# Seven-product matmuls for two output projections, with new sequence cuts, in a hybrid decoder block

## Chip, cores, metric

One Trainium2 chip, all 8 cores, one launch. The metric is the device time of the slowest core in microseconds (us). The time is in most executions within 0.3% of the median; in some a whole die runs at a lower granted clock, and such a run is called slow.

Four names of kinds of core are used throughout, because the program is a switch over four variants: cores 0/4, 1/5, 2/6 and 3/7 compute the first, second, third and last quarter of a sequence, for batch 0 (cores 0 to 3) and batch 1 (cores 4 to 7). A later quarter has more keys to attend to, so it gets fewer tokens. Which quarter is how long is set by the constant `CUTS`.

## The reference, cut

```python
# D_MODEL 2048, SEQ 4096 + 16 meta tokens, 8 heads of 128, conv width 1024, D_FF 8192
xn = rms_norm(h, norm_mix)
q, k, v, fg, cb, cc, cx, gl = split(xn @ w_in)         # one combined projection
a = forgetting_attention(rms(q), rms(k), v, log_sigmoid(fg + b)) @ w_attn_out   # 1024 -> 2048
c = (cb * short_conv(cc * cx, conv_w)) @ w_conv_out                             # 1024 -> 2048
ga, gc = split(sigmoid(gl + b_gate))                   # two gates of 2048
h = h + (ga * a + gc * c) @ w_o
h = h + square(relu(rms_norm(h, norm_mlp) @ w_up)) @ w_down
```

## The kernel before

Each core runs through these stages: projections for q, k, v; attention; convolution; gates together with the two output projections; `w_o` (called `o`); and the MLP. All large products with an inner width of 2048 or more already use a seven-product scheme of the Strassen kind: a product of 2x2 blocks is made of 7 block products in place of 8, for some sums of weights (`wsum`) and of operands (`lincomb`), which VectorE makes in f16. The two output projections, whose inner width is 1024, were plain: four quadrant products of 8 matmuls per pair of column blocks, called `plain` below.

```python
CUTS = [0, 1200, 2264, 3240, L]
...
def lincomb(nm, kb, extra=()):          # operand sums, on VectorE
    def sub(out, a, b, w=()): S.op("dve", lambda e: e.tensor_tensor(..., op=ALU.subtract), ...)
    return [lambda: sub(JT3, J22, J12[nm]), lambda: sub(JT1, J12[nm], J11, ...),
            lambda: sub(JT2, J22, JT1), lambda: sub(JT4, J21, JT2)]

def taps(j):                            # depthwise convolution of width 3
    S.op("act", lambda e: e.activation(out=y[:], in_=ub[:, 0:n + 2], func=AF.Identity, scale=cw(0)), ...)
    for t in (1, 2):
        S.op("dve", lambda e, t=t: e.scalar_tensor_tensor(out=y[:], in0=ub[:, t:t + n + 2], scalar=cw(t), in1=y[:], ...), ...)
...
groups7 += [("g", "xn", kG(p, g), (g, p)) for p in range(8) for g in range(2)]     # gates
groups7 += [("o", "m7", K_O + 2 * p, (0, p)) for p in range(8)]
...
class Group:
    def P1(self): self.prod(self.X, self.wa[:, 0:8], [self.ka], J11, True); self.copy(p1_t, p1k)
    def P7(self): self.sprod(self.Y, 3, JT3, True)      # sprod: a product with a weight sum
    def P6(self): self.sprod(self.X, 2, JT2, False); self.copy(us_t, usk)
    def P2(self): self.prod(self.Z, self.wa[:, 8:16], [self.ka], J21, True)
    ...                                                 # P5, P3, P4 likewise
    def plain(self, q, sl=None):
        def mm(e):
            for x in range(NP):
                for kb in range(8):
                    rhs = cT[kb][:, lo:lo + fw] if g else aT[:, kb, q0 + lo:q0 + lo + fw]
                    ins = e.matmul(ps[sl[x]][:, 0:fw], lhsT=w[:, 8 * s + kb, :], rhs=rhs, start=(kb == 0), stop=(kb == 7))
        S.op("pe", mm, ...)
        tt_op(wide(sv_[g]), pv(sl, fw), wide(sv_[g]), ALU.mult, ...)       # gate times product
        if g: tt_op(operand["m7"](j, p), sv_[0], sv_[1], ALU.add, ...)     # the two branches
...
def fin(self, s, half):                 # stage o: operand and square of a finished row
    S.op("act", lambda e: e.activation(out=operand["x7"](j, self.b), in_=ht, func=AF.Identity, ...), ...)
    S.op("act", lambda e: e.activation(out=sq2[q][:], in_=ht, func=AF.Square), ...)
    pend.append(ssq)                    # the matmul that sums the squares is put off
def flush(keep):
    while len(pend) > keep: pend.pop(0)()
```

`NP` is 2 on cores 0, 1, 4, 5, whose rows are split in two matmuls, and 1 on the others. A solver places all tiles in the on-chip memory; tiles that find a place early (`soon`) can be filled while attention still runs.

Of the kernel before, what the change touches and what calls it, by code (L numbers as in the profile page):

```python
# [14 lines left out]
L = SEQ + NMETA  # L15
# [9 lines left out]
CUTS = [0, 1200, 2264, 3240, L]  # L25
# [3 lines left out]
WMAX = 1200  # L29
W0 = 490  # L30
NTW = 24 + 48 + 16 + 128
K_G, K_O, K_F, NR = 24, 72, 88, 6
# [236 lines left out]
T_V, T_K, T_ATT, T_C0, T_G, T_GE, T_OE, T_END = 12, 14, 16, 20, 24, 30, 35, 99  # L269

def solve(want, busy, movable, hpair):
# [4 lines left out]
    for it in range(400):  # L276
        used = list(busy)

        def put(nb, t0, t1):
            live = sorted((a, b) for a, b, s0, s1 in used if s0 < t1 and t0 < s1)  # L280
            x = O_A
            for a, b in live:
                if x + nb <= a:
                    break
                x = max(x, b)
            if x + nb > TOP:
                return None
            used.append((x, x + nb, t0, t1))
            return x
        place, soon = {}, set()  # L290
        for w in first + sorted(rest, key=lambda w: -prio[w[0]]):
            x = put(w[3], movable[w[0]], w[5]) if w in first and w[0] in movable else None
            if x is not None:
                soon.add(w[0])
            else:
                x = put(w[3], w[4], w[5])
            if x is None:
                prio[w[0]] *= 1.5
                break
            place[w[0]] = x  # L300
# [23 lines left out]
def emit(nc, sems, T, psall, ps, G, S0, g0):  # L324
# [155 lines left out]
    for h in range(H):  # L480
        S.reg(("QT", h), "QT", o_Q + h * 2 * W, o_Q + (h + 1) * 2 * W)
        for c in range(nch):
# [10 lines left out]
    busy = [(O_A, o_A1, 0, T_C0), (o_A1, o_rs, 0, T_C0), (o_rs, o_xog, 0, 9), (o_xog, o_R, 0, T_GE), (o_R, o_H, 0, T_V), (o_wk, o_wk + 32768, 0, T_K),  # L493
            (o_K, o_Q, 0, T_ATT), (o_K, o_K + 4096, 0, T_C0), (o_Q, o_end, 0, T_GE)] + ([(o_x, o_V, 0, T_K), (o_V, o_K, 0, T_ATT)] if early else [(o_x, o_K, 0, T_ATT)])
    J11, J21, J22, JT1, JT3, JT2, JT4 = range(7)
    BASE, EXT = (J11, J21, J22, JT1), (JT3, JT2, JT4)
    NSS, NZ, NSQ = 6, 3, 3
# [3 lines left out]
    J12 = {nm: 7 if nm == "xn" and apart else JT1 for nm in ("xn", "m7", "x7", "u7")}  # L501
# [3 lines left out]
    def ask(name, shape, dtype, t0, t1, keys):  # L505

        want.append((name, shape, dtype, r32(int(np.prod(shape)) * (2 if dtype in (BF16, F16) else 4)), t0, t1, keys))
    f32s = lambda nm, k, w, t0, t1: [ask("%s%d" % (nm, i), [w], F32, t0, t1, [(nm, i)]) for i in range(k)]
    op7 = lambda nm, x, w, js, t0, t1: [ask("%s%s%d_%d" % (nm, x, kb, j), [w], F16, t0, t1, [(nm, j, kb)]) for kb in range(8) for j in js]
    ask_h = lambda i: [ask("hp%d_%d" % (i, s), [n], F32, T_GE, T_END, [("hp", i, s, c) for c in range(2)]) for s in range(2)]  # L510
    for i in range(NR):
        ask("ring%d" % i, [2048], F16, T_V, T_END, [("ring", i)])
    f32s("ub", 1, 2 * TC, T_K, T_G)
    f32s("yb", 1, n + 2, T_K, T_G)
    f32s("cx", 2, TC, T_K, T_G)
    op7("xn", "e", TC, EXTX, T_ATT, T_GE)
    ask("yb1", [n + 2], F32, T_S, T_G, [("yb", 1)])
    for i in range(NSS):
        ask("swt%d" % i, [8, 128], F16, T_S, T_END, [("swt", i)])
    for nm in ("p1", "us", "tt"):  # L520
        f32s(nm, 1, TC, T_S, T_END)
    for j in range(8):
        ask("cT%d" % j, [n + 2], F16, T_S if j < 2 or apart else T_C0, T_GE, [("cT", j)])
    for g in range(2):
        f32s("sg%d" % g, 4, TC, T_G, T_GE)
    op7("m7", "b", TH, BASE, T_G, T_OE)
    op7("x7", "b", TH, BASE, T_GE, T_END)
    op7("x7", "e", TH, EXT, T_GE, T_END)
    op7("u7", "b", TH, BASE, T_OE, T_END)
    op7("u7", "e", TH, EXT, T_OE, T_END)  # L530
    ask("rstd_m", [n], F32, T_OE - 1, T_END, [("rstd_m", c) for c in range(2)])
    f32s("zz", NZ, TH + 8, T_GE, T_END)
    for i in range(2):
        ask_h(i)
    op7("m7", "e", TH, EXT, T_GE, T_OE)
    assert not apart or n <= 1000
    place, soon, nhp = solve(want, busy, {w[0]: T_G if w[0][:3] == "m7e" else T_K for w in want if w[0][:3] in ("m7e", "xne")}, (r32(4 * n), T_GE, T_END))
# [7 lines left out]
    soon7 = [all("xne%d_%d" % (kb, x) in soon for x in EXTX) for kb in range(8)]  # L545
    xcol = {J11: (0, c0), J12["xn"]: (0, c0 + TC), J21: (8, c0), J22: (8, c0 + TC)}
# [4 lines left out]
    operand = {nm: (lambda j, kb, nm=nm: tl["%s%s%d_%d" % (nm, "b" if j in BASE else "e", kb, j)][:]) for nm in ("m7", "x7", "u7")}  # L551
    operand["xn"] = lambda j, kb: xog[:, xcol[j][0] + kb, xcol[j][1]:xcol[j][1] + TC] if j in xcol else tl["xne%d_%d" % (kb, j)][:]
# [3 lines left out]
    rstd_m, z_t, hp = tl["rstd_m"], tls("zz", NZ), [tls("hp%d_" % i, 2) for i in range(nhp)]  # L556
    zz = lambda i: place["zz%d" % i]
    ssb = M.at("ssb", [128, TH], F32, zz(2))[0]
    S.reg("ssb", "ssb", zz(2), zz(2) + 4 * TH)
    sq2 = [M.at("sq2%d" % i, [128, TH], BF16, zz(i // 2) + i % 2 * r32(2 * TH))[0] for i in range(NSQ)]  # L560
    for i in range(NSQ):
        S.reg(("sq2", i), "sq2%d" % i, zz(i // 2) + i % 2 * r32(2 * TH), zz(i // 2) + i % 2 * r32(2 * TH) + 2 * TH)
# [592 lines left out]

    def xn_sum(kb, j):
        lincomb("xn", kb, xn_extra(kb))[j]()
        S.lastw.update({("xn", b, kb): ("dve", S.sem["dve"], S.cnt["dve"]) for b in xcol if b != JT1})
# [114 lines left out]
    plain_r = Ring([(0, 1)] if NP == 2 else [(0,), (1,), (2,), (3,)])  # L1273
    s_bank, b_bank = ((0, 1), [(0, 1), (0, 1)]) if NP == 2 else ((0,), [(1,), (2,)])

    kG = lambda p, g: K_G + (2 * g if p == 0 else 6 * p - 1 + 3 * g)
    groups7 = [(kd, "xn", 2 * i, (a, b)) for i, (kd, a, b) in enumerate(CONV) if i]
    NCV = len(groups7)
    groups7 += [("g", "xn", kG(p, g), (g, p)) for p in range(8) for g in range(2)]
# [12 lines left out]
    sw_r, z_r = Ring(list(range(NSS))), Ring(list(range(NZ)))  # L1292
    sums = {}

    def wsum(i, j):

        if i >= NG7:
            return
        k = groups7[i][2]
        assert k + 1 < wt_n[0], (i, k, wt_n[0])  # L1300
        wa, wb, ka, kb_ = wview(k), wview(k + 1), wkey(k), wkey(k + 1)
        sl = sums.setdefault(i, {})
        s = sl[j] = sw_r.next()
        t = lambda x: swt[sl[x]][:]
        a, b, op, rk = {1: lambda: (wb[:, 0:8], wb[:, 8:16], ALU.add, [kb_]),
                        2: lambda: (t(1), wa[:, 0:8], ALU.subtract, [ka, ("swt", sl[1])]),
                        3: lambda: (wa[:, 0:8], wb[:, 0:8], ALU.subtract, [ka, kb_]),
                        4: lambda: (wa[:, 8:16], t(2), ALU.subtract, [ka, ("swt", sl[2])])}[j]()
        tt_op(swt[s][:], a, b, op, rk, [("swt", s)])
# [10 lines left out]
    class Group:  # L1320
        def __init__(self, i):
# [3 lines left out]
            self.turn = (self.kind, nxt) in (("g", "o"), ("o", "u"), ("u", "d"), ("d", None))  # L1325
# [4 lines left out]
            self.cost = 8 * self.T / 2400  # L1330
            self.four = (NP == 1 and i >= NTAIL) or self.kind in ("u", "d")

        def begin(self):
            if self.four:
                self.X, self.Y, self.Z, free = slots
                if self.turn and self.kind in ("u", "o"):
# [5 lines left out]
            self.wa, self.wb = wview(self.k), wview(self.k + 1)  # L1342
            self.ka, self.kb = wkey(self.k), wkey(self.k + 1)

        def prod(self, d, w, wkeys, j, start, kbs=range(8)):
            f = self.f

            def mm(e):
                for p in range(NP):
                    for kb in kbs:  # L1350
                        ins = e.matmul(ps[d[p]][:, 0:f], lhsT=w[:, kb, :], rhs=self.op(j, kb)[:, p * f:(p + 1) * f],  # L1351
                                       start=(start and kb == 0), stop=(kb == 7), skip_group_check=not start)
# [21 lines left out]
        def up(self, src, keys, add, addk, half, j):  # L1374
            z = z_r.next()
            zk = ("zz", z)
            if add is not None:
                tt_op(wide(z_t[z][:, 0:TH]), src, wide(add[:, 0:TH]), ALU.add, keys + [addk], [zk])
                src, keys = wide(z_t[z][:, 0:TH]), [zk]
# [483 lines left out]
```

## Time and profile before

| | before |
|---|---|
| time, median of the first 5 runs | 1968.43 us (1967.19 to 2140.8) |
| TensorE busy, page of core 7 | 1891.9 us, 96% of the span |
| VectorE busy | 1227.4 us, 62% |
| ScalarE busy | 844.6 us, 43% |
| spans, cores 0 to 3 | 1911.8, 1944.8, 1942.1, 1964.3 us |

How to read it: TensorE sets the end, and the last quarter's cores are the slowest by 19 us. The prediction shows the lines for this. The view of windows has columns window, length, then busy time and instruction count of TensorE, its weight loads, VectorE, ScalarE and GpSimd, then granted clock of TensorE, DMA share and GB/s. First core 4 in its convolution stage:

```profile
334.00:521.00 187.00, 179.17 (x1423) 136.29 (x1424) 126.19 (x241) 46.94 (x72) 12.16 (x23) 0.99 0.41 68
```

TensorE is busy 179 of 187 us at a clock of 0.99. Then core 7 around the end of attention, which is at 813 us:

```profile
764.00:790.00 26.00, 24.50 (x182) 13.61 (x179) 18.75 (x50) 18.49 (x38) 1.06 (x2) 1.00 0.14 24
790.00:815.00 25.00, 21.39 (x141) 11.35 (x142) 15.93 (x28) 12.61 (x25) 1.05 (x2) 1.00 0.26 45
815.00:836.00 21.00, 15.50 (x76) 7.64 (x74) 14.59 (x41) 3.17 (x6) 1.05 (x2) 0.84 0.29 49
```

The first 51 of these 72 us run at the full clock; only after the end of attention does it fall to 0.84.

### The profile page before, as it was taken

The page shows a single profiled execution, that of the slowest core. Times are in us where ns is not written, and L with a number is a line of the kernel's source. Part 1 is how long each engine was busy: PE and PEld are TensorE (multiplying, and loading weights), DVE is VectorE, ACT ScalarE, POOL GpSimd, SP SyncE. Part 2 cuts the span into 40 slices and gives each one's busy share as a digit, 9 for nine tenths or more (in the row PEclk, how much of TensorE's full clock was granted, in tenths as well). Part 3 has the DMA queues.
Part 4 walks back from the last instruction along what each step waited for, and adds up shares of the span by engine and source line. Part 5 has one row for each costly group of instructions (what it writes and reads, how often), then busy time and mean ns, then how long its engine had stood idle before and what let it go on. Part 6 is the DMA issues. An engine that isn't in the chain of part 4 may idle for free.

```text
span 1964.4 us, 39987 instructions; the slowest of 8 cores (1911.8 to 1964.4 us)
## 1 busy us (share of the span) xinstructions
PE 1891.9 (96%) x13096; PEld 1165.0 (59%) x13096; DVE 1227.4 (62%) x2712; ACT 844.6 (43%) x1734; POOL 131.3 (7%) x254
## 2 busy tenths in 40 slices
PE   6899999999999999799999998999999999999998
PEld 2478677777777776455555554445555555555554
DVE  3534566666666655677455555667667767766765
ACT  4325667777777777322222223443113212312321
POOL 1100000000000000010000000001011001100110
PEclk9999999999999999999999999999999999999999
DMA  9840333323333314255465568866786787688676
GB/s 223 151 70 2 115 112 109 98 87 106 99 100 110 107 55 73 47 98 96 78 103 99 96 102 188 209 140 108 176 210 102 134 200 158 101 205 181 107 156 187
DMA packets 68035, 240.49 MB, mean 122 GB/s; under 512 B 7920, under 2 KB 8048, under 8 KB 67440
## 3 DMA queue, kind: packets, MB, share of 16 engines
q0 software_dynamic: 34128, 125.94, 38.3%
q1 hardware_dynamic: 33696, 111.89, 17.4%
q8 instruction: 114, 1.87, 0.4%
q14 instruction: 97, 0.79, 0.1%
HBM read 338.73 MB, written 25.00 MB: 185 GB/s over the span
## 4 chain that ended last, share of the span: by engine, by line
PE 87%; DMA 4%; DVE 3%; issue 2%; ACT 2%; SPq 0%; DVEq 0%; POOL 0%; ACTq 0%; POOLq 0%
PE ps L1351 49%; PE ps L801 12%; PE ps L837 11%; PE ps L1564 5%; PE ps L1098 5%; PE ps L1069 5%; DMA wq<-wqk 1%; DMA v_wv<-wv 1%; DMA x<-xo 1%; ACT v_PT L1084 1%; DMA v_hp<-xt 1%; DMA v_xs<-xo 0%; PE ps L1184 0%; DVE v_swt L1291 0%; ACT v_sq L1391 0%
## 5 line engine op out<-in xcount | busy, mean ns | idle before, releaser
L1084 ACT ACTIVATE v_PT<-ps,v_small 128x104 bf16<-128x104 f32 (+2 forms) x752 | 395.4, 577 | 165.2 <-PE ps L1098 86.2
L1126 DVE SCALAR_TENSOR_TENSOR v_acc<-ps,v_small,v_acc 128x387 f32<-128x387 f32 (+1 forms) x312 | 164.9, 529 | 144.4 <-PE ps L1069 106.0
L165 POOL DMA_DIRECT2D v_ring<-wB x216 | 114.0, 529 | 1708.3 <-PE ps L1351 834.5
L1069 PE MATMUL ps<-v_QT,v_KT 128*128 128x104 bf16 (+2 forms) x752 | 202.6, 281 | 10.6 <-ACT v_PT L1084 9.8
L837 PE MATMUL ps<-v_xg,v_wk 128*128 128x256 f16 (+1 forms) x1664 | 209.9, 269 | 0.5 <-DVE v_xg L996 0.5
L801 PE MATMUL ps<-v_wv,v_xg 128*128 128x387 f16 (+1 forms) x1248 | 210.0, 310 | 0.0
L1098 PE MATMUL ps<-v_VB,v_PT 128*128 128x129 bf16 (+1 forms) x1632 | 196.6, 220 | 7.2 <-DVE v_acc L1126 3.5
L1291 DVE TENSOR_TENSOR v_hp<-ps,v_hp 128x436 f32<-128x436 f32 x160 | 97.3, 608 | 135.4 <-PE ps L1351 130.5
L837 PEld LDWEIGHTS ps<-v_xg,v_wk 128*128 128x128 f16 x1664 | 150.0, 98 | 18.6 <-issue 0.6
L1382 ACT ACTIVATE v_u7b<-v_zz 128x436 f16<-128x436 f32 x128 | 72.5, 567 | 201.3 <-DVE v_zz L1380 201.3
L1098 PEld LDWEIGHTS ps<-v_VB,v_PT 128*128 128x128 bf16 (+1 forms) x1632 | 126.9, 97 | 41.0 <-issue 14.4
L1364 ACT COPY v_us<-ps 128x436 f32<-128x436 f32 (+1 forms) x99 | 51.1, 516 | 223.9 <-PE ps L1351 216.4
L801 PEld LDWEIGHTS ps<-v_wv,v_xg 128*128 128x128 f16 x1248 | 114.6, 98 | 49.9
L1351 PE MATMUL ps<-v_xne,v_swt 128*128 128x438 f16 x648 | 132.9, 348 | 2.7 <-ACT v_us L1364 1.5
L1351 PE MATMUL ps<-v_u7b,v_ring 128*128 128x436 f16 x512 | 105.4, 347 | 0.5
L1351 PE MATMUL ps<-v_x7b,v_swt 128*128 128x436 f16 x512 | 104.7, 347 | 0.9 <-ACT v_tt L1364 0.5
L1351 PE MATMUL ps<-v_u7b,v_swt 128*128 128x436 f16 x512 | 104.7, 347 | 0.8 <-ACT v_tt L1364 0.8
L1351 PE MATMUL ps<-v_x7b,v_ring 128*128 128x436 f16 x512 | 104.9, 347 | 0.0
L1351 PE MATMUL ps<-v_u7e,v_swt 128*128 128x436 f16 x512 | 104.1, 347 | 0.0
L1351 PE MATMUL ps<-v_x7e,v_swt 128*128 128x436 f16 x512 | 104.1, 347 | 0.0
L1351 PEld LDWEIGHTS ps<-v_xne,v_swt 128*128 128x128 f16 x648 | 62.2, 98 | 59.2 <-issue 6.0
L1364 ACT COPY v_tt<-ps 128x436 f32<-128x436 f32 (+1 forms) x99 | 50.9, 514 | 104.4 <-PE ps L1351 103.4
(173 smaller groups left out, 2926.6 us busy)
## 6 DMA issues: line engine op xcount, KB each, us to landing
v_ring<-wB POOLq DMA_DIRECT2D x216, 512.0 KB, 6.8
v_stage<-xe SPq DMA_DIRECT2D x52, 512.0 KB, 3.7
v_stage<-xr SPq DMA_DIRECT2D x52, 512.0 KB, 3.9
hd<-v_hp SPq DMA_DIRECT2D x40, 436.0 KB, 6.4
v_hp<-hd SPq DMA_DIRECT2D x40, 436.0 KB, 7.4
v_hp<-xt SPq DMA_DIRECT2D x16, 436.0 KB, 8.5
y<-v_hp SPq DMA_DIRECT2D x16, 436.0 KB, 5.7
wq<-wqk POOLq DMA_DIRECT2D x8, 512.0 KB, 14.4
```

Of the source, the lines that this page charges most:

```text
L165: self.eng[q].dma_start(out=out, in_=in_).then_inc(sem, 16)
L801: ins = e.matmul(ps[b][:x.shape[-1], 0:nh * 129], lhsT=x, rhs=wv_t[hg][:, kc, :], start=(kc == 0), stop=(kc == KC - 1))
L837: ins = e.matmul(ps[b][:, 0:N], lhsT=wk[:, h, kc, :], rhs=cols(kc), start=(kc == 0), stop=(kc == KC - 1))
L1069: ins = e.matmul(ps[sb][:, 0:N], lhsT=KT[ks][:, koff:koff + 128], rhs=QT[:, h, lo:hi], start=True, stop=not diag)
L1084: S.op("act", lambda e: e.activation(out=PT[pt][:m, 0:N], in_=ps[st["s"]][:m, 0:N], func=AF.Exp, bias=small[:m, bcol:bcol + 1], scale=smal ...
L1098: ins = e.matmul(ps[ob][:, k * 129:(k + 1) * 129], lhsT=PT[pt][:m, ql - lo:ql - lo + 128], rhs=Vt[vs][:m, h, :], start=(first and b == bl[ ...
L1126: S.op("dve", lambda e, ov=ov, av=av, mq=mq, fc=fc: e.scalar_tensor_tensor(out=av, in0=ov, scalar=small[:mq, fc:fc + 1], in1=av, op0=ALU.m ...
L1291: tt_op = lambda out, a, b, op, rk, wk_: S.op("dve", lambda e: e.tensor_tensor(out=out, in0=a, in1=b, op=op), reads=rk, writes=wk_)
L1351: ins = e.matmul(ps[d[p]][:, 0:f], lhsT=w[:, kb, :], rhs=self.op(j, kb)[:, p * f:(p + 1) * f], start=(start and kb == 0), stop=(kb == 7), ...
L1364: S.op("act", lambda e: e.copy(out=wide(t[:, 0:self.T]), in_=self.pv(self.X)), reads=bks(self.X), writes=[key])
L1382: S.op("act", lambda e: e.activation(out=operand["u7"](j, self.b), in_=z_t[z][:, 0:TH], func=AF.Square), reads=[zk], writes=[("u7", j, sel ...
L1564: ins = e.matmul(ps[sl[x]][:, 0:fw], lhsT=w[:, 8 * s + kb, :], rhs=rhs, start=(kb == 0), stop=(kb == 7))
```

## The change

Its intent: both output projections go through the seven-product scheme as well, 7 products of 4 matmuls per pair in place of 4 of 8, so 448 matmuls for 512 (896 for 1024 where `NP` is 2). This needs operand sums and weight sums of its own, a new memory layout (the solver gets a hand-written plan), an order of weights with all attention projections ahead of the gates, and lists that put additions off to quieter places. At the same time the sequence is cut anew, the last quarter gets 20 tokens fewer, and stage `o` may hold two squares back in place of one.

```diff
-CUTS = [0, 1200, 2264, 3240, L]
+CUTS = [0, 1216, 2280, 3260, L]
...
-    NSS, NZ, NSQ = 6, 3, 3
+    NSS, NSQ = 6, 4
...
+    op7("a7", "e", TH, EXT, T_C0, T_G, 4)
+    op7("c7", "e", TH, EXT, T_G, T_GE + 1, 4)
+    plan = [("ring", o_R)] + [("swt%d" % i, o_R) for i in range(4)] + [(x, o_R) for x in ("p1", "us", "tt", "cT1", "ub", "yb0", "cx", "xne")]
...
-    groups7 += [("g", "xn", kG(p, g), (g, p)) for p in range(8) for g in range(2)]
+    groups7 += [("a", "a7", K_A + p, (0, p)) for p in range(8)]
+    groups7 += [x for p in range(8) for x in (("g", "xn", K_G + 5 * p, (0, p)), ("g", "xn", K_G + 5 * p + 2, (1, p)), ("c", "c7", K_G + 5 * p + 4, (0, p)))]
...
+            self.w = 4 if self.kind in ("a", "c") else 8
-            self.four = (NP == 1 and i >= NTAIL) or self.kind in ("u", "d")
+            self.four = i >= NTAIL if NP == 1 else i >= 4 and self.kind != "o"
...
+        def merge_(self, q, src, keys, add=None, addk=None):
+            if add is not None:
+                tt_op(wide(add[:, 0:TH]), src, wide(add[:, 0:TH]), ALU.add, keys + [addk], [addk])
+                src, keys = wide(add[:, 0:TH]), [addk]
+            tt_op(wide(self.sg(1, q)), src, wide(self.sg(1, q)), ALU.mult, keys + [k1], [k1])
+            out = (lambda: tt_op(operand["m7"](QJ[q], self.b), self.sg(0, q), self.sg(1, q), ALU.add, ...))
+            if self.turn: out()
+            else: adds.append(out)
...
-        def plain(self, q, sl=None):
-            ...
-        fl = [(0, lambda: flush(1))] if prev and prev.kind == "o" else []
+        fl = [(0, lambda: flush(2))] if prev and prev.kind == "o" else []
...                         # order of the packed weights
     for p in range(8):
+        half(w_ao, p)
+    for p in range(8):
         for g in range(2):
             ...
-        half(w_ao, p)
-    half(w_co, 7)
+        half(w_co, p)
```

## The prediction

> **What bounds the kernel now.** I read the page of the slowest core first, then the view of all cores, because the program is a switch over four variants (cores 0/4, 1/5, 2/6, 3/7 hold the first to the last quarter of a sequence) and the time is that of the slowest core.
>
> ```profile
> span 1964.4 us, 39987 instructions; the slowest of 8 cores (1911.8 to 1964.4 us)
> PE 1891.9 (96%) x13096; PEld 1165.0 (59%) x13096; DVE 1227.4 (62%) x2712; ACT 844.6 (43%) x1734; POOL 131.3 (7%) x254
> PE 87%; DMA 4%; DVE 3%; issue 2%; ACT 2%; SPq 0%; DVEq 0%; POOL 0%; ACTq 0%; POOLq 0%
> ```
>
> TensorE is busy for 96% of the span and is 87% of the chain that ended last. VectorE at 62% has room on average.
>
> ```profile
> core 4: 1913.3 us, clock 0.993
> core 5: 1945.9 us, clock 0.994
> core 6: 1945.2 us, clock 0.994
> core 7: 1964.4 us, clock 0.994
> ```
>
> The variants are not level: the last is 19 us above cores 5 and 6 and 51 above core 4. So what a change saves on cores 3/7 beyond 19 us is worth nothing unless cores 1, 2, 5 and 6 get faster too. I therefore put cores 6 and 7 side by side over their stages: gates (with the two output projections) and the stage of the projection `o`; the rows give busy time per engine and, with x, its instructions.
>
> ```profile
> 807.00:1086.00 279.00, 279.00 (x1353) 131.43 (x1352) 132.53 (x209) 68.54 (x108) 24.25 (x46) 1.00 0.48 84
> 1086.00:1193.00 107.00, 100.66 (x465) 45.17 (x464) 71.67 (x137) 45.43 (x81) 8.46 (x16) 0.97 0.83 206
> ...
> 941.00:1190.00 249.00, 249.00 (x1350) 131.75 (x1348) 131.64 (x228) 62.44 (x107) 24.25 (x46) 1.00 0.55 94
> ```
>
> First and second row core 6, third core 7. In the gate stage TensorE never stops: 279 us for 1352 matmuls (one in the window's count is a border case) is 206.4 ns each at 488 to 490 columns; on core 7 249/1350 is 184.4 ns at 436 to 438. VectorE works 132.5 of 279 us there. So every matmul taken out of this stage is worth its full pace, as long as VectorE and ScalarE keep up.
>
> The rows by shape give the prices (core 6):
>
> ```profile
> L1564 PE MATMUL ps<-v_aT,v_ring 128*128 128x488 f16 x256 | 57.9, 368 | 0.0
> L1564 PE MATMUL ps<-v_cT,v_ring 128*128 128x488 f16 x256 | 57.7, 369 | 0.0
> L1291 DVE TENSOR_TENSOR v_sg<-ps,v_sg 128x488 f32<-128x488 f32 x64 | 42.5, 665 | 87.3 <-PE ps L1564 86.4 <-ACT v_sg L1408 1.0
> L1291 DVE TENSOR_TENSOR v_swt<-v_ring,v_ring 128x1024 f16<-128x1024 f16 x99 | 67.7, 684 | 2.8 <-DMA v_ring<-wB 2.8
> L1150 DVE TENSOR_TENSOR v_u7e<-v_u7b,v_u7b 128x488 f16<-128x488 f16 x64 | 26.2, 409 | 6.1 <-ACT v_u7b L1382 3.2
> L1364 ACT COPY v_p<-ps 128x488 f32<-128x488 f32 x72 | 40.0, 556 | 45.0 <-DVE v_hp L1291 35.8 <-PE ps L1351 9.2
> ```
>
> The first two rows are what goes: the plain products, 512 on this core. VectorE waited 86 us for them, so it had slack. And TensorE's waits, core 6 within its `o` stage, then one row of core 7's whole list:
>
> ```profile
> PE ps L1351 <- DVE v_m7e L1150: 3.5, 1, 3.5
> PE ps L1396 <- ACT v_sq L1391: 2.5, 6, 0.4
> ...
> PE ps L1396 <- ACT v_sq L1391: 8.8, 8, 5.1
> ```
>
> At the turn from gates to `o`, TensorE waits for operand sums or for squares. That is the stall which the change's side edits address.
>
> **What the Trainium skill says.** "TensorE: Matmul & The Clock Gate", section "Wait — 56ns, not 53.3ns?", has N/2.4 GHz plus about 2.5 ns start to start. For 437 columns that is 184.6, for 489 it is 206.3: the trace agrees (184.4, 206.4). The section "Back-to-back issue gap" of the same page claims 131 ns at N=512 for real streams; this trace contradicts it. "Perfetto Trace Analysis", section "Identifying the Most-Contended Engine", warns that matmul busy time misleads; indeed the row says 368 ns for one matmul that is paced at 206, so I count columns and not busy time. "VectorE: DVE Perf Modes", section "The perf-mode tier table (the rule you actually need)", has tensor_tensor at two 16-bit elements a cycle in SBUF and one for fp32 or PSUM: 1024 f16 in 684 ns against 488 f32 in 665 agrees.
>
> **The change part by part.**
>
> 1. *Strassen-like products for both output projections.* Before, each is 4 quarter products of 8 matmuls for each of 8 column pairs. After, 7 products of 4 matmuls with twice the reach: for both projections 512 matmuls become 448 (twice that on cores 0, 1, 4, 5, which split rows in two). Saved: 64 x 488 columns on core 6, which is 64 x 206 ns = 13.2 us; core 7 64 x 184 = 11.8; core 5 128 x 113 = 14.5; core 4 128 x 126 = 16.1. The cost of the sums is on VectorE and ScalarE: 144 more VectorE and 56 more ScalarE instructions on every variant (counted in the two built programs). On core 6: 64 half-wide weight sums, estimated at 418 ns (684 less 512 elements at 0.52 ns, the slope between the 1024 and 488 rows), 27 us; 32 operand sums of 409 ns, 13 us; 48 added PSUM reads of 665 ns, 32 us. ScalarE 56 x 556 ns = 31 us. Gate-stage VectorE then rises from 132 to about 200 of some 270 us, 74%; ScalarE to 100.
>
> 2. *New cuts*, 1216, 1064, 980, 852 tokens for 1200, 1064, 976, 872. Counting output columns of all matmuls in the two builds, with part 1 included: core 0 kind 4,271,000 to 4,287,848; core 1 kind 4,324,024 to 4,292,024; core 2 kind 4,375,056 to 4,360,068; core 3 kind 4,330,272 to 4,232,828. At 1/2.4 ns a column and 2.5 ns for each matmul fewer (128, 128, 64, 64): +6.7, -13.7, -6.4 and -40.8 us. So 4 tokens more eat half of core 6's gain: 13.2 saved, 6.8 added.
>
> 3. *Queue and buffer edits.* Four square buffers for three and two squares left pending for one; sums of the turn brought forward; one scratch tile for three in the MLP (the sum is made in place); a fourth PSUM slot on cores 0, 1, 4, 5. The turn's waits above are 6.0 us on core 6, and after a wait of 3.5 us the next matmuls there ran at half pace (clock 0.97 in that row). I put the gain in the `o` stage at 6 us on each core, of the 6.3 us that TensorE is idle in core 6's row and 9.7 in core 7's. In the MLP I expect nothing: the ScalarE square already stood ahead of the next copy in the same queue.
>
> 4. *New waits.* A product of 4 matmuls lasts 0.83 us on core 6 and 0.72 on core 7. I walked the order of the built program. From the product that ends the first quadrant to the one that needs the next weight sum there are 2 products (1.65 and 1.44 us), and in between VectorE does one PSUM add and one half sum: 0.67 + 0.42 plus an estimated 0.3 for tail and semaphore, 1.4 us on core 6 and 1.3 on core 7. It holds, narrowly on core 7. In the conv group itself VectorE has about 7 us of work for 5.8 of TensorE, but the next gate group has 11.6 us to absorb it, and I found a slack of a microsecond. So I put down 2 us of new waits on core 6, 3 on core 7.
>
> Sum, from the profiled spans: core 4: 1913 + 7 - 6 + 2 = 1916. Core 5: 1946 - 14 - 5 + 2 = 1929. Core 6: 1945 - 6 - 6 + 2 = 1935. Core 7: 1964 - 41 - 6 + 3 = 1920. The slowest becomes core 2/6 at 1935. The timed median stands 4 us above the profiled span (1968.4 against 1964.4), of which I keep 3: **1938 us**, 1.5% less than before.
>
> **The rivals.**
> - *VectorE lags in the short groups.* For it: 74% on average with bursts above 100%, in-order queue, core 3/7 narrowest. Against: slack of about a microsecond in my walk. If each of 16 short groups waited 0.7 us, that is 11 us: core 6 at 1944, core 7 at 1929, time 1947.
> - *The cuts were right because cores 2/6 gain more than I see.* Whoever gave core 2 four tokens more should have found it fast. If the turn loses all its stalls (10 us in the stage) and no new waits come, core 6 is 1929 and the time 1931; just short of 2%.
> - *Weight traffic.* The attention-projection groups eat one 512 KB tile in 5.8 us, at most the rate of the MLP (two in 11.6), where VectorE waited 2.8 us in all for a tile (the weight-sum row above). I give it little.
> - *The time follows core 7.* Then it would fall by 44 us, over 2%. The view of cores speaks against: cores 5 and 6 stand in between.
>
> **Range and chances.** 1926 to 1948 holds the sums with the stall terms at their ends. 2% less is 1929: it needs core 6 to gain 16 to 19 us where I count 10, chance 0.17. Slower by 2% would need 40 us of new waits on all variants, 0.02. Within 2%: 0.81.
>
> **What would show it.** In the profile after: gate-stage TensorE still above 97% busy and VectorE near 74% (step 1, 4); cores 2 and 6 the longest, cores 3 and 7 near 1920 (step 2); the wait for squares below 2 us and none above 2 us at the turn to `o` (step 3). I am wrong if TensorE's waits for weight sums or PSUM reads exceed 8 us in a gate stage, or if cores 2 and 6 stand below 1928.

## The result, and the profile after

| | before | after |
|---|---|---|
| time, median | 1969.56 us (15 runs, 1965.12 to 2140.8) | 1939.23 us (9 runs, 1937.29 to 2007.32) |
| ratio after to before | | 0.9845, 95% interval 0.9833 to 0.9858 |

Ratios are the mean time of one kernel's fast runs over the mean of the other's fast runs of the same rounds, so not quite the ratio of the medians quoted. The kernel is 1.55% faster, within 2%, and the time is 1.2 us above the predicted 1938.

The page after, by its slowest core, which is now core 2:

```profile
span 1937.9 us, 36192 instructions; the slowest of 8 cores (1928.3 to 1937.9 us)
...
PE 1883.3 (97%) x11704; PEld 1061.9 (55%) x11704; DVE 1272.0 (66%) x2664; ACT 804.3 (42%) x1522; POOL 131.9 (7%) x255
...
PE 90%; DMA 4%; DVE 3%; issue 1%; ACT 1%; SPq 0%; POOL 0%; DVEq 0%; ACTq 0%; POOLq 0%
```

TensorE's share rose from 96 to 97% and its part of the last chain from 87 to 90%. VectorE went from 62 to 66%. (The page before is of core 7 and this one of core 2, so these shares are of two different programs.) The view of all cores after, for the four cores that the prediction showed:

```profile
core 4: 1928.3 us, clock 0.995
core 5: 1930.3 us, clock 0.997
core 6: 1935.3 us, clock 0.998
core 7: 1935.5 us, clock 0.991
```

The four are within 7.2 us, where they were 51 apart. The single profile is one run; the medians of the fast runs, both cores of a kind taken together, say more (before: the 8 fast runs of later runs on one chip; after: 8 fast runs):

| kind of core | before | after | change | predicted change |
|---|---|---|---|---|
| 0/4 | 1913.6 | 1931.2 | +17.6 | +3 |
| 1/5 | 1945.4 | 1934.4 | -11.0 | -17 |
| 2/6 | 1946.0 | 1935.0 | -11.0 | -10 |
| 3/7 | 1965.8 | 1931.3 | -34.5 | -44 |

So the kind that was predicted to set the time came out as predicted, and three others did not. The rest of this document is mostly about those.

The stages that the prediction put side by side, core 6 after, view of windows:

```profile
794.00:850.00 56.00, 53.63 (x260) 24.69 (x258) 37.57 (x77) 19.30 (x34) 4.24 (x8) 1.00 0.51 86
850.00:1078.00 228.00, 227.76 (x1098) 106.99 (x1097) 160.78 (x289) 82.89 (x135) 21.20 (x40) 1.00 0.54 91
1078.00:1181.00 103.00, 98.55 (x470) 45.04 (x469) 73.14 (x132) 46.36 (x82) 8.49 (x16) 1.00 0.82 207
```

The first two rows are the gate stage, now split into the attention projection and the gates with the convolution's projection, the third is stage `o`. In the second, TensorE is busy 227.76 of 228 us; in the first it lost 2.4 us; both together have VectorE at 198 of 284 us, 70%, where it was 48%. In stage `o` the row went from 107 to 103 us and its clock from 0.97 to 1.00. TensorE's waits in stage `o` of core 6 after (us in total, times, longest):

```profile
PE ps L1400 <- ACT v_tt L1413: 1.9, 1, 1.9
PE ps L1400 <- DVE v_m7e L1174: 1.6, 1, 1.6
PE ps L1400 <- DVE v_tt L1326: 0.8, 1, 0.8
```

The waits for squares (line of ScalarE's `v_sq`) are gone; 4.3 us remain, from what feeds the turn. Two groups of core 6 after, the new weight sums and one of the new products (view of lines by shape):

```profile
L1400 PE MATMUL ps<-v_a7e,v_swt 128*128 128x490 f16 x64 | 15.8, 369 | 2.4 <-DVE v_swt L1326 2.4
...
L1326 DVE TENSOR_TENSOR v_swt<-v_ring 128x512 f16<-128x512 f16 x32 | 12.0, 418 | 0.0
```

The half-wide weight sum takes 418 ns, as the prediction had estimated from the slope between two other rows.

**An account by stage.** To see where each kind differs from its sum, I tabulated from the trace, for each stage, the time from its first matmul's start to the next stage's, less its matmuls' columns at 1/2.4 ns and 2.5 ns each. What is left is TensorE's lost time: waits, lowered clock, tails. In us, profiled fast runs, before and after. (After, the convolution stage ends earlier in the order of groups, so it is taken together with the gates.)

| lost time, before / after | core 4 | core 5 | core 6 | core 7 |
|---|---|---|---|---|
| projections | 34.7 / 32.2 | 34.6 / 34.9 | 33.3 / 32.7 | 38.1 / 40.4 |
| attention | 20.5 / 17.0 | 26.1 / 25.6 | 28.6 / 30.2 | 52.2 / 59.9 |
| convolution and gates | 14.9 / 35.2 | 17.7 / 18.1 | 9.1 / 11.1 | 12.0 / 16.5 |
| `o` | 13.0 / 7.5 | 9.3 / 7.7 | 11.7 / 6.2 | 14.1 / 9.2 |
| MLP | 13.0 / 12.6 | 14.1 / 13.5 | 9.6 / 8.6 | 10.4 / 12.7 |
| sum of changes | +8.4 | -2.0 | -3.5 | +11.9 |
| columns (prediction, step 2) | +6.7 | -13.7 | -6.4 | -40.8 |
| span in this profile | +15.0 | -15.6 | -9.9 | -28.9 |

The sum of changes and the columns add up to the span within 0.1 us. Lost time is what the columns leave, so this must come out; it shows only that the columns counted in the built programs are those of the traces. That the price is right shows elsewhere: in the gate stage of the kernel before, where TensorE never stopped, the lost time of cores 6 and 7 is 0.0 us. What went astray is lost time: 20 us in the convolution and gates of core 4, and 10 in the first two stages of core 7. (How much of this is chance: four profiles of core 3 whose code is the same up to the gates, of the changed kernel, its repeat and two experiments below, have 57.5 to 60.5 us in attention and 36.3 to 41.5 in the projections. So the 2.3 us in core 7's projections say nothing.) The waits of core 4 around its convolution stage, and that stage's row in the view of windows:

```profile
PE ps L1400 <- DVE v_swt L1326: 9.0, 2, 7.9
PE ps L1400 <- DVE v_xne L1174: 6.1, 1, 6.1
```

```profile
330.00:516.00 186.00, 165.76 (x1280) 122.98 (x1280) 132.01 (x270) 41.33 (x65) 11.84 (x22) 0.96 0.36 60
```

Two waits on VectorE of 6.1 and 7.9 us stand here that the kernel before doesn't have (there no wait of VectorE in this stretch was above 1.7 us), and the clock of the stretch is 0.96 for 0.99. On core 7 the same view at the end of attention:

```profile
790.00:815.00 25.00, 20.63 (x123) 10.39 (x122) 13.50 (x23) 12.45 (x24) 1.05 (x2) 0.86 0.15 25
815.00:840.00 25.00, 18.80 (x89) 9.45 (x90) 15.51 (x43) 3.87 (x7) 1.06 (x2) 0.80 0.30 47
```

Set beside the rows of before, the clock now falls 25 us sooner (from 764 to 790 us it is still 1.00). TensorE's wait there, in the list of waits of core 7 and, for its twin core 3, in the order of time on TensorE and on VectorE:

```profile
PE ps L1122 <- DVE v_acc L1150: 9.3, 4, 4.3
```

```profile
820.86 0.49 PE L1122 MATMUL ps<-v_VB,v_PT 128*128 128x129 bf16 x2 [4.28 <-DVE v_acc L1150]
```

```profile
817.86 2.32 DVE L1200 SCALAR_TENSOR_TENSOR v_yb<-v_ub,cst,v_yb 128x854 f32<-128x854 f32 x2 [1.31 <-ACT v_yb L1198]
820.10 1.79 DVE L1150 SCALAR_TENSOR_TENSOR v_acc<-ps,v_small,v_acc 128x387 f32<-128x387 f32 x3
```

TensorE stood still 4.28 us for an accumulation of attention (`v_acc`). VectorE was not working on it: two convolution taps stood ahead of it in the program, and the first of them was itself held 1.31 us by ScalarE's part of the tap (`v_yb`). VectorE kept to the program's order and stood idle through these 1.31 us, although TensorE, idle since 816.6 us, had delivered every product that the accumulations needed. In the kernel before the last such pair of taps came after the last accumulations; core 7 before, on VectorE:

```profile
813.32 1.07 DVE L1126 SCALAR_TENSOR_TENSOR v_acc<-ps,v_small,v_acc 128x387 f32<-128x387 f32 x2 [1.40 <-PE ps L1098]
816.97 2.37 DVE L1165 SCALAR_TENSOR_TENSOR v_yb<-v_ub,cst,v_yb 128x874 f32<-128x874 f32 x2 [1.33 <-ACT v_yb L1163]
```

### The profile page after: what moved, and what is told of

Its sections match the earlier page's. It is cut to its first block, busy times and chain, and to the rows that moved or that the text cites. A ratio compares the mean times of both kernels' runs of the same rounds, so it can differ in the third digit from the quotient of the medians.

```text
span 1937.9 us, 36192 instructions; the slowest of 8 cores (1928.3 to 1937.9 us)
## 1 busy us (share of the span) xinstructions
PE 1883.3 (97%) x11704; PEld 1061.9 (55%) x11704; DVE 1272.0 (66%) x2664; ACT 804.3 (42%) x1522; POOL 131.9 (7%) x255
## 4 chain that ended last, share of the span: by engine, by line
PE 90%; DMA 4%; DVE 3%; issue 1%; ACT 1%; SPq 0%; POOL 0%; DVEq 0%; ACTq 0%; POOLq 0%
PE ps L1400 61%; PE ps L825 9%; PE ps L861 9%; PE ps L1122 4%; PE ps L1093 4%; DMA wq<-wqk 2%; DMA v_wv<-wv 1%; DMA x<-xo 1%; PE ps L1219 1%; DMA v_xs<-xo 1%; DVE v_yb L1200 1%; PE ps L1444 0%; DVE v_swt L1326 0%; ACT v_yb L1198 0%; DVE v_atk L1277 0%
## 5 line engine op out<-in xcount | busy, mean ns | idle before, releaser
L1108 ACT ACTIVATE v_PT<-ps,v_small 128x212 bf16<-128x212 f32 (+5 forms) x568 | 316.0, 604 | 126.4 <-PE ps L1093 61.4
L1150 DVE SCALAR_TENSOR_TENSOR v_acc<-ps,v_small,v_acc 128x387 f32<-128x387 f32 (+2 forms) x288 | 139.1, 483 | 87.0 <-PE ps L1122 39.4
L1093 PE MATMUL ps<-v_QT,v_KT 128*128 128x212 bf16 (+4 forms) x568 | 164.1, 295 | 2.4 <-ACT v_PT L1108 1.2
L1400 PE MATMUL ps<-v_xne,v_swt 128*128 128x492 f16 x648 | 148.1, 372 | 1.2 <-DVE v_cT L1326 0.7
L1400 PE MATMUL ps<-v_u7b,v_swt 128*128 128x490 f16 x512 | 116.3, 370 | 0.9 <-ACT v_tt L1413 0.9
L1400 PE MATMUL ps<-v_u7b,v_ring 128*128 128x490 f16 x512 | 116.9, 370 | 0.0
L1400 PE MATMUL ps<-v_x7b,v_swt 128*128 128x490 f16 x512 | 116.3, 370 | 0.3 <-ACT v_tt L1413 0.3
L1400 PE MATMUL ps<-v_x7b,v_ring 128*128 128x490 f16 x512 | 116.4, 370 | 0.0
L1400 PE MATMUL ps<-v_u7e,v_swt 128*128 128x490 f16 x512 | 115.6, 370 | 0.0
L1400 PE MATMUL ps<-v_x7e,v_swt 128*128 128x490 f16 x512 | 115.6, 370 | 0.0
L1413 ACT COPY v_p<-ps 128x490 f32<-128x490 f32 (+1 forms) x115 | 64.4, 560 | 79.1 <-DVE v_hp L1326 34.5
```

The source lines that it names most:

```text
L1093: ins = e.matmul(ps[sb][:, 0:N], lhsT=KT[ks][:, koff:koff + 128], rhs=QT[:, h, lo:hi], start=True, stop=not diag)
L1108: S.op("act", lambda e: e.activation(out=PT[pt][:m, 0:N], in_=ps[st["s"]][:m, 0:N], func=AF.Exp, bias=small[:m, bcol:bcol + 1], scale=smal ...
L1150: S.op("dve", lambda e, ov=ov, av=av, mq=mq, fc=fc: e.scalar_tensor_tensor(out=av, in0=ov, scalar=small[:mq, fc:fc + 1], in1=av, op0=ALU.m ...
L1400: ins = e.matmul(ps[d[p]][:, 0:f], lhsT=w[:, kb, :], rhs=self.op(j, kb)[:, p * f:(p + 1) * f], start=(start and kb == 0), stop=(kb == self ...
L1413: S.op("act", lambda e: e.copy(out=wide(t[:, 0:self.T]), in_=self.pv(self.X)), reads=bks(self.X), writes=[key])
```

## The experiments

Nine runs were made; one of them repeats the changed kernel and one repeats another experiment. Five were on two chips with mostly fast executions; four were on a chip whose second die was slow in every execution, the kernel before included (2101 us), and of those only the undisturbed cores 0 to 3 are read.

### Products and side edits without the new cuts

The changed kernel with the old cuts:

```diff
-CUTS = [0, 1216, 2280, 3260, L]
+CUTS = [0, 1200, 2264, 3240, L]
-WMAX = 1216
+WMAX = 1200
```

> The changed kernel with the old cuts (1200, 1064, 976, 872 tokens), so the new products and buffers alone. By columns at 1/2.4 ns and 2.5 ns a matmul, cores 0/4, 1/5, 2/6, 3/7 save 16, 14, 13 and 12 us. Theory A, that what cores 3/7 lost against my sum (1937 seen, 1920 predicted) comes mostly with the new cuts (columns taken where columns do not set the pace): cores 3/7 at 1964 - 12 - 4 (o stage) + 5 (short groups) = 1953, time about 1957. Theory B, that the new code itself costs cores 3/7 their 15 us whatever the cuts: 1963 or more, time as before. Cores 0/4: if the loss there (1930 seen, 1916 predicted) comes with the new layout, which no longer has room for the early operand sums, its stall of some 15 us before the transposes stays with the old cuts: 1912 - 16 - 4 + 15 = 1907; if it comes with the wider core, 1892.

Measured: 1957.47 us, ratio 0.9947 (0.9927 to 0.9966), all 4 runs fast. By kind of core, medians, with the kernel before on the same chip in the first column (4 fast runs):

| kind | before | old cuts, new products | after | products and side edits | cuts on top | columns of the cuts |
|---|---|---|---|---|---|---|
| 0/4 | 1914.5 | 1908.5 | 1931.2 | -6.0 | +22.7 | +22.8 |
| 1/5 | 1944.2 | 1934.7 | 1934.4 | -9.5 | -0.3 | +0.8 |
| 2/6 | 1945.7 | 1929.6 | 1935.0 | -16.1 | +5.4 | +6.8 |
| 3/7 | 1965.5 | 1954.9 | 1931.3 | -10.6 | -23.6 | -29.0 |

(The last column is step 2's columns less step 1's products: 6.7 + 16.1 for the first row.) Three things follow. The products alone are worth 0.5%, because cores 3/7 stay in front; the cuts make 1.5% of it. The cuts cost or give what their columns say, except on cores 3/7, which lose 5 of 29 us. And the missing time of cores 0/4 is there with the old cuts already: the products gave 6 us where 20 had been summed, so it isn't the width. The waits of core 4 in this run show the same two entries, 6.1 us for `v_xne` and 9.4 for weight sums. The cuts can't be tried the other way round, on the kernel before: its solver finds no place for all tiles with the first quarter at 1216, so it does not build ("no layout"). The new layout is what makes the new cuts possible.

### The new cut of the last quarter alone

The kernel before with 852 tokens on cores 3/7. Its output is wrong: the 20 rows that no core computes are filled with others (relative error 0.095).

```diff
-        self.A, self.B = CUTS[p], CUTS[p + 1]
+        self.A, self.B = (3260 if p == 3 else CUTS[p]), CUTS[p + 1]
...
+        if p == 3: out[b, a - 20:a, :] = y[:, :20].T
```

> The kernel before with the last quarter alone shortened from 872 to 852 tokens (20 rows of the output are wrong on purpose). By columns cores 3/7 save 69,540 columns, 29 us: 1964 to 1935. Theory A says that the columns of the projection stage (2.4 us) and of the attention stage (some 2 us, paced by ScalarE and VectorE) buy nothing, and the end of attention may stall more: saving 20 to 24 us, 1940 to 1944. Rival: the full 29, 1935; then the loss is the new code's. Cores 0, 1, 2 unchanged, so the time is that of cores 1 and 5, some 1948.

Measured: 1951.72 us, two fast runs, cores 3/7 at a median of 1942.0, so 23.5 us less, of the 29 that the columns give. Cores 2/6, the same code as before, are at 1944.7. The lost time of core 7 grew by 2.7 us in the projections and 5.0 in attention and by 1.3 in `o`. TensorE's wait for `v_acc` at the end of attention went from 3.5 to 7.6 us, its longest from 1.8 to 4.3. With the old cuts and the new products it was 4.7, longest 2.6. So the long wait comes from the shorter quarter: the program mixes attention and convolution by their estimated costs, and with the new width a pair of taps falls ahead of the last accumulations (in this run's trace too: taps at 813.83 us, the last three accumulations at 816.07). The long wait is not the whole loss, though. The run with the old cuts and the new products, which does not have it, lost 4.1 us more in attention than the kernel before on core 7 (56.3 for 52.2) and 4.7 on core 3, and core 7's clock falls early there as well: 0.86 from 790 to 815 us. So the new code costs something here by itself; which of its edits does it was not tested.

### Late operand sums in the kernel before

With the new layout only 7 of the convolution's operand-sum tiles of cores 0/4 find an early place, where 24 did. A block's sums are made early only if all three of its tiles have one, so in the changed kernel all of them come late (`soon7` is false for every block). If that is what costs, the kernel before must show it when its sums are made late:

```diff
     soon7 = [all("xne%d_%d" % (kb, x) in soon for x in EXTX) for kb in range(8)]
+    if G.p == 0:
+        soon7 = [False] * 8
```

> The kernel before, with the operand sums of the shared input on cores 0/4 put behind the attention instead of among the first conv products, as the layout of the changed kernel forces them. If that is what costs cores 0/4 their 15 us: 1912 rises to 1925 to 1929, its conv stage from 187 to some 203 us, with waits for operand sums and weight sums of 6 and 7 us where before none is above 2. Rival, the wider core does it: 1912 to 1914.

Measured: time 1970.17, as before, since cores 3/7 set it (two runs; in the profiled one cores 0 and 1 were disturbed, at clocks of 0.977 and 0.981, so core 4 is read). Its span was 1924.6 us, against 1913.3 in the profile of before, so 11.3 us more (in the second run cores 0 and 4 stood at 1924.5 and 1927.0). The convolution stage of core 4 took 204.0 us for 187.4, with a lost time of 30.1 us, against 13.5 before and 28.3 in the changed kernel. Its wait:

```profile
PE ps L1353 <- DVE v_xne L1152: 19.3, 1, 19.3
```

It is one wait of 19.3 us, not two of 6 and 7 as I had expected: the sums form one burst here and are split by weight sums in the changed kernel. The size fits, the shape does not. Of the 14 us that cores 0/4 gained too little, this accounts for about 11. The rest is 5.5 us of lost time in the gate stage of core 4 (1.4 to 6.9), where I had 2.

### The taps one at a time

The changed kernel, with the two VectorE parts of a tap issued singly, at later points, on cores 2, 3, 6, 7:

```diff
-            S.op("dve", lambda e, t=t: e.scalar_tensor_tensor(out=y[:], ...), ...)
+            tapq.append(lambda t=t: S.op("dve", lambda e, t=t: e.scalar_tensor_tensor(out=y[:], ...), ...))
+        if NP == 2 or not split: tap(2)
...
+ run_list(acts) + [(0.1, lambda: tap(1))]          # after product 6
+ C("P2") + [(0.1, lambda: tap(1))] + E("P2e")      # after product 2
```

> The changed kernel, with the two VectorE convolution taps of a group issued one at a time, later, instead of both at once ahead of the attention's accumulations, on cores 2, 3, 6, 7. Theory: these taps (2.3 us in the in-order queue) keep the accumulator waiting, the tensor engine idles 2.1, 2.4 and 4.4 us and its clock is halved after it (0.86 and 0.80 granted). Then waits for v_acc on core 3 fall from 9.6 to below 4 us, the granted clock of cores 3 and 7 rises to 0.995 or more, core 3 falls from 1937 to about 1927 and core 2 from 1938 to about 1932; time about 1935, as cores 0 and 1 at 1931 then matter. Rival: the wait only moves on to the next operand that the same queue delivers, as the kernel before has a gap of 4.6 us just after the attention; then cores 2 and 3 stay within 3 us of 1937.

Measured: 1940.32 us, ratio 0.9861 (0.9842 to 0.9881), so the same as the changed kernel. Cores 3/7 have a median of 1928.3 for 1931.3; cores 2/6, which had been expected near 1932, have 1934.7 for 1935.0. In the profiled runs core 3's lost time in attention fell from 60.5 to 54.2 us. The wait and the clock of core 7, rows that answer to those of the changed kernel:

```profile
PE ps L1122 <- DVE v_acc L1150: 4.5, 3, 2.3
```

```profile
790.00:815.00 25.00, 20.89 (x125) 10.57 (x126) 13.48 (x24) 12.29 (x25) 0.95 (x2) 0.86 0.19 34
815.00:840.00 25.00, 20.64 (x113) 10.83 (x113) 18.70 (x50) 4.56 (x9) 1.75 (x4) 0.93 0.40 68
```

The second row's clock is 0.93 for 0.80; the first keeps its 0.86. What happens in it, on TensorE, in order of time:

```profile
792.18 0.33 PE L1122 MATMUL ps<-v_VB,v_PT 128*128 128x129 bf16 x3 [2.25 <-DVE v_acc L1150]
...
793.10 2.88 PE L1409 MATMUL ps<-v_xne,v_swt 128*128 128x428 f16 x8
...
796.90 1.61 PE L1409 MATMUL ps<-v_xne,v_swt 128*128 128x428 f16 x8
```

After standing still for 2.25 us, a group of 8 matmuls of 428 columns takes 2.88 us, and the next one of the same 8 takes 1.61. So the wait was paid a second time, with 1.3 us, by a slower clock (granted 0.50 from 793.3 to 796.7 us). That need not follow: in the later run of both repairs, below, core 7 has the same wait of 2.25 us before 788.90, the clock stays at 1.00 from 764 to 815 us, and the same group takes its full pace:

```profile
789.94 1.61 PE L1409 MATMUL ps<-v_xne,v_swt 128*128 128x428 f16 x8
```

What decides between the two was not tested. The theory holds for the wait; the time does not move, since cores 1/5 and 2/6 are then in front.

### How much slack VectorE has in the short groups

One more idempotent VectorE operation (a maximum of a tile with itself) after every read of a product of the convolution's projection, 32 in all:

```diff
             tt_op(wide(self.sg(1, q)), src, wide(self.sg(1, q)), ALU.mult, ...)
+            for _ in range(1):
+                tt_op(self.sg(1, q), self.sg(1, q), self.sg(1, q), ALU.max, [k1], [k1])
```

> The changed kernel with one more VectorE instruction (maximum of a gate tile with itself, no effect on the result) after each of the four multiplications of a conv-projection group: 32 instructions of about 0.6 to 0.78 us, 20 us of VectorE work in the gate stage. Theory (my prediction's walk): VectorE has a slack of about 1 us in a conv group on cores 2/6 and 0.4 us on cores 3/7, so of the 2.4 to 2.7 us added per group some comes through: gate stage 4 to 8 us longer on cores 2/6, 8 to 12 us on cores 3/7. Rival 1, VectorE already binds there: nearly all 20 us come through. If it has more slack than I found: below 2 us on all.

The chip of this run had one slow die throughout; in the unchanged repeat of the changed kernel, the median of the first die's cores is 1937.4 us at a clock of 0.994, that of the second 2076.6 us at 0.917.

> The changed kernel once more, on the chip and in the rounds of the others: 1937 to 1941 us; medians by kind of core near 1931, 1934, 1935, 1931, with jumps of 7 us up on cores 1/5 and 3/7 from run to run.

The repeat's undisturbed cores, medians of 8 runs, are 1932.7, 1932.3, 1936.5 and 1933.5 us (one of the 8 had the first die slow too; without it they fall by 0.4 us at most), so within 2.2 us of the fast runs of the changed kernel; its times prove nothing more. Against it, the gate stage with the extra operations:

| core | extra VectorE work | gate stage | longer by |
|---|---|---|---|
| 0 | 32 x 784 ns = 25.1 us | 352.4 to 363.7 us | 11.3 us |
| 1 | 32 x 714 ns = 22.8 us | 312.0 to 327.5 us | 15.5 us |
| 2 | 32 x 670 ns = 21.4 us | 283.7 to 302.5 us | 18.8 us |
| 3 | 32 x 604 ns = 19.3 us | 250.9 to 272.4 us | 21.5 us |

and TensorE's new waits on core 2:

```profile
PE ps L1400 <- ACT v_tt L1413: 11.3, 8, 1.6
PE ps L1400 <- DVE v_swt L1326: 5.4, 7, 0.8
```

I had expected 4 to 12 us; the rival, that VectorE is at its edge in these groups, is nearer. By the busy time of the added operations there is no slack at all on core 3, and on core 2 it is (21.4 - 18.8) / 8 groups = 0.3 us a group. On core 3 more came through than was added: the view of lines puts 3.7 us of idle time before these operations there and 3.3 on core 2. Counting that as added, the slack is 0.2 us a group on core 3 and 0.7 on core 2. The share of 70% in the gate stage tells nothing of this: in the short groups a read, its sums and the next weight sum stand in one chain.

### One square pending

The changed kernel with `flush(1)` again:

```diff
-        fl = [(0, lambda: flush(2))] if prev and prev.kind == "o" else []
+        fl = [(0, lambda: flush(1))] if prev and prev.kind == "o" else []
...
-            st += [(0, lambda: flush(2))]
+            st += [(0, lambda: flush(1))]
```

> The changed kernel with one square left pending in the o stage instead of two, as before the change (the four buffers stay). Theory (step 3): the repeated waits for squares, 0.6 us a group, come back: o stage 3 to 5 us longer on cores 2/6 and 3/7 (102 to 106 and 93 to 98 us), with waits for v_sq of 2 us or more in sum. Rival: the gain in the o stage came from the turn alone, then the stage stays within 1 us.

Measured on cores 0 to 3, stage `o`: 128.5, 117.0, 106.8 and 98.9 us, against 126.6, 113.6, 102.6 and 95.1 in the repeat, so 1.9 to 4.2 us more. On core 2 the wait for squares is back:

```profile
PE ps L1444 <- ACT v_sq L1439: 3.8, 7, 1.4
```

So of the 5 us that stage `o` of core 6 gained, this one edit makes most. On cores 0/4, where the stage gained 5.5 us, it makes 1.7 (9.2 us of lost time on core 0, for 7.5); which side edit gave the rest was not tried.

### Both repairs together

The changed kernel with the taps apart, and on cores 0, 1, 4, 5 the weight sums ahead of the late operand sums:

```diff
-        rest7.append((0, lambda: wsum(0, 3)))
+        rest7 += [(0, lambda j=j: wsum(0, j)) for j in (3, 1, 2, 4)]
         ...                                                  # the late operand sums
-        rest7 += [(0, lambda j=j: wsum(0, j)) for j in (1, 2, 4)]
```

> The taps-apart kernel, and on cores 0/1/4/5 the four weight sums of the first product group put ahead of the late operand sums. Theory: on cores 0/4 the weight sums no longer queue behind 32 operand sums; the wait of 7.7 us falls to about 4, conv stage 187 to 183 us, span 1930 to 1926; cores 1/5 unchanged, since their sums are early. The time is set by cores 1, 2, 5, 6 and is then 1937 to 1940, same as the changed kernel. It would beat it only if cores 0/4 were often the last.

This run fell on the chip with the slow die. Its undisturbed cores had medians of 1929.2, 1931.0, 1934.5 and 1927.2, against 1932.7, 1932.3, 1936.5 and 1933.5 of the repeat. It was run again:

> The same kernel as apart_sums_first, whose run fell on a chip with one die in the slow state and gave no verdict on time; here again for the time. Theory A (the time is the highest of eight cores that are now level, and each kind of core has its own small repairable wait): by the medians of the undisturbed die in that run, [1929, 1931, 1935, 1927] against [1933, 1932, 1937, 1934] of the changed kernel, the time of a fast run comes to 1935 to 1939 us, 1 to 4 us under the changed kernel's 1939, a ratio to the kernel before of 0.982 to 0.985. Rival (cores 2 and 6, which neither edit touches, set the time alone): within 1 us of the changed kernel.

Measured: 1939.14 us (5 fast runs), ratio to before 0.9845 (0.9831 to 0.986): the same as the changed kernel. By kind: 1929.0, 1934.9, 1934.2, 1928.7. The rival was nearer. The two repaired kinds are 2 to 3 us faster, the other two are where they were, and the mean of the fast times went from 1939.6 to 1938.2, which the interval doesn't tell from nothing. On core 4 the wait for weight sums fell from 9.0 to 1.2 us, but the wait for operand sums rose from 6.1 to 11.3: the burst is nearly as long as it was, in another order (the convolution stage took 182.9 us for 186.0). No version that beats the changed kernel was found.

## Why the prediction was right, and where it was not

Cores 2/6 came out as predicted because for these the sum held nearly term by term: columns -6.4, stage `o` -5.5 for -6, new waits +2.0 for +2. The last agreement is partly luck: the gate stage alone lost 3.5 us more, and the convolution, for which the sum had no term, 1.5 less. What else was not in it, +1.6 us in attention, -0.6 in the projections and -1.0 in the MLP, cancels. That the time agrees to 1.2 us is luck as well, for it does not hang on cores 2/6 alone: the longest core of the 8 fast runs is of kind 2/6 in three, of 1/5 in four and of 3/7 in one. Taken by its steps:

1. *Products.* Right in price: the counted columns are those of the traces, and where TensorE never stops they leave 0.0 us. VectorE's share in the gates was put at 74% and is 70%; TensorE was to stay above 97% there and is busy 281.4 of 284 us.
2. *Cuts.* The columns are right; the step fails where it turns them into time. On cores 3/7 it took 40.8 us of columns for 40.8 us of span. The lost time of core 7 grew by 10.0 us ahead of the convolution, where the shorter quarter saves but 4.1 us of columns. Of the 7.7 us in attention, 5.7 went away with the taps apart, so most of it is shown: a pair of taps ahead of three accumulations, and the clock. But the two parts of the change do not add up there: the shorter quarter alone cost 5.0 us in attention and the new code alone 4.1, and the second is not explained. Cores 3/7 stand at 1931, not near 1920.
3. *Queues.* Mis-sized by little: `o` gained 5.5, 1.6, 5.5 and 4.9 us on cores 4 to 7, where I wrote 6, 5, 6 and 6. Waits for squares are gone, and the longest wait in core 6's `o` is 1.9 us, under the 2 that the prediction named as its test. On cores 3 and 7 the test fails: one wait for `v_tt`, 13 us into the stage, is 2.8 and 2.7 us.
4. *New waits.* With the convolution counted in, right in size on core 6 and fairly on core 7 (4.5 us for 3); in the gate stage alone too small, 3.5 us for 2 and 6.8 for 3. The "slack of a microsecond" was too high: the extra operations found 0.3 to 0.7 us on core 2 and none to 0.2 on core 3. The walk's own figures, 1.65 us against 1.4 and 1.44 against 1.3, had said so. (Two sums among the rivals are off by one: 1920 - 3 + 11 is 1928, not 1929, and 1929 + 3 is 1932, not 1931.)

What no step had is the memory. The diff's new plan was read for what it makes possible, not for what it pushes out: 17 operand-sum tiles of cores 0/4 lost their early place, and this step is missing from the sum (+2 of new waits, where convolution and gates lost 20.3 us). It cost nothing in the time, as these cores were to end 19 us below the slowest; it used up all but 4 of them.

The 3 us between profile and time had a wrong reason. The time is the highest of eight cores that jitter: before, it stood 3.1 us over the median of cores 3/7, which were alone in front (1968.9 against 1965.8); after, with all four kinds level, 4.6 us over that of cores 2/6 (1939.6 against 1935.0). In both kernels 1.5 us of this lie between the longest core and the time, so the jitter's part went from 1.6 to 3.1 us. That the repairs of single kinds bought nothing is the same thing seen from the other side.

Open: cores 1/5 are at a median of 1934.4 where 1929 was predicted, though their profiled run, at 1930.3, fits the sum. Their runs spread from 1928.8 to 1945.3 us. In one profile with core 5 at 1938.1 it waited 4.3 us for residual tiles (`v_hp`) in the MLP, a wait that isn't in the profile at 1930.3. The kept traces bear this out: in the repeat, core 1 at 1941.2 us has 25.2 us of lost time in the MLP, for 13.4 in the profile at 1930.6, which is more than its whole excess; VectorE waited there up to 10.0 us at once for the loads of `v_hp`, for 3.7. Why these loads come late in some executions stays open. The 2.3 us that core 7 lost more in the MLP was not tested either.

## What to carry to other kernels

Price a change in matmul columns per core, but credit the columns as time only in stages where TensorE has no lost time; in the others, look first at what VectorE's in-order queue will put ahead of the result that TensorE waits for. When a change adds tiles to a full memory, list which tiles lose their early place on every variant: a share of busy time shows neither that nor the slack in a short chain. When all cores are level, repairing one kind buys nothing, and the time stands some microseconds above the highest median.

## What the Trainium skill lacked or had wrong

- "TensorE: Matmul & The Clock Gate", section "HAM oscillation — how this bites in real kernels", gives the rule that idle gaps of TensorE over about 3.4 us bring the lower clock. Here a gap of 2.25 us was enough on core 7 with the taps apart: the granted clock was 0.50 for the next 3.4 us, 8 matmuls of 428 columns in it took 2.88 us, and the following 8 took 1.61. With both repairs the same gap left the clock at 1.00, so the length of the gap alone does not tell.
- The same page, section "Seeing it yourself", says to budget 1.95 GHz (13/16 of the clock) once three cores of a die run dense matmuls. In the fast runs of the changed kernel all eight cores did so at mean granted clocks of 0.991 to 0.999. The slow die of the repeat, at means of 0.907 to 0.924, does show the page's level, but in pieces: core 4 was granted 0.81 from 1294.3 to 1302.2 us, 1.00 to 1308.9 and 0.81 again to 1320, in all 968 of 2091 us. The page says that the limit holds while the load lasts; that it comes and goes under a steady load, and in some executions only, no page was found to say.
- The same page's figure of 131 ns for a sustained matmul at N=512 (section "Back-to-back issue gap"), which the prediction had found contradicted, is contradicted after the change as well: the gate stage of core 6 in the second row of its windows has 1098 matmuls in 228 us, 207 ns each at 490 to 492 columns.
